# Where the weight tiles of a decoder step lie in SBUF: halves 2,176 bytes apart instead of 2,048, and three gaps

## The chip, the cores and the metric

The kernel runs on one core of a Trainium2 chip, as one program with one launch. The metric is the device time of one execution in microseconds (us); before and after are compared by the median of several executions. A profile is one further execution, recorded by the hardware profiler. Its engines are TensorE (PE for the matmuls, PEld for the weight loads that go with them), VectorE (DVE), ScalarE (ACT), GpSimd (POOL) and SyncE (SP, which here only issues DMAs). Everything is computed in 32-bit floats.

## The reference

One step of a decoder layer on 288 tokens (256 of a prompt, 32 of a sample), model width 2,048: an FFN, a mixer of two kinds of gated linear recurrences, and a second FFN, each between two RMS norms.

```python
x = x + 0.5 * rmsnorm(swiglu(rmsnorm(x, g[0]), ffn1_w_in[l], ffn1_w_out[l]), g[1])
m, sg, sh = hybrid_mixer(rmsnorm(x, g[2]), mix_w_in[l], ...)      # proj = h @ w_in; scans; merged @ w_out
x = x + rmsnorm(m, g[3])
x = x + 0.5 * rmsnorm(swiglu(rmsnorm(x, g[4]), ffn2_w_in[l], ffn2_w_out[l]), g[5])
# swiglu: gate, up = split(x @ w_in); (silu(gate) * up) @ w_out, with hidden width 5,632
```

Nearly all of the arithmetic is in the products with the weights: 2,048 x 11,264 and 5,632 x 2,048 in each FFN, about 2,048 x 7,168 and 2,048 x 2,048 in the mixer. In blocks of 128 x 128 these are 5,376 weight blocks.

## The kernel before

**Weights.** Each weight is read from memory once, in units of 1,024 columns on 128 partitions (`raw`, 512 KB). A unit holds two blocks of rows (two values of `k`), each 512 columns wide. `Weights.pieces` (L85 to L99) splits a unit into a high part `wh`, which ACT rounds to the matmul's format (L96), and a low part `wl`, the rest, which DVE subtracts (L97). 676 instructions on each engine do this over the whole kernel. The tiles come from a pool `hlp` with four buffers of each; at the two borders between stages (FFN 1 to mixer, mixer to FFN 2) some units take theirs from a second pool `hx`, on the right side of the memory, which lives only around the border.

**Products.** The activations are split in the same way into `xh` and `xl` (in the FFN's second half `hh` and `hl`). A product is then three matmuls: high by high, low by high, high by low (L591, L592, L593 in `mm3`). Each loads a 128 x 128 weight block into TensorE and streams 288 columns of a moving tile past it. 5,376 blocks by three, and 24 more at the two borders, make 16,152 weight products. In this document a *weight product* is one such matmul with its weight load.

**Order.** `block` runs over units, over the two `k` of a unit, and over four column blocks `f`: twelve weight products in a row use the tiles `xh[k]` and `xl[k]`, and the next twelve those of `k + 1`. In the last unit of a block (the *tail*) `f` is the outer loop: three products with one `k`, three with the next. A `gate` or `up` block of an FFN has sixteen `k`, so 168 products in runs of twelve and 24 in the tail; an `out` block has four `k`, 24 in two runs of twelve and 24 in the tail. The engines' order is the order in which the code issues, except where `issue_after` places instructions behind others.

**Borders.** `Fill` (from L506) holds eight pairs of early-split tiles (`xh`, `xl`, `yh`, `yl` for `k` from 0 to 3) whose products are put into the wait for the norm at each border. `Border` opens the pools for them.

**Layout.** Each partition of SBUF is one row of bytes, and pools lay their tiles one behind the other. These are the start addresses of the built program, modulo 256 bytes:

- An activation tile has 288 x 4 = 1,152 bytes, which is 4 x 256 + 128. So `xh[k]` and `xl[k]` start at 64 for even `k` and at 192 for odd `k`.
- `hh` and `hl` have four such slices in 4,608 = 18 x 256 bytes; the slices start at 0, 128, 0, 128.
- A weight tile has 4,096 bytes, and a weight block starts every 512 bytes in it. All 15,480 products with weights from `hlp` load them from 192, the 672 with weights from `hx` from 224.
- The `Fill` tiles start at 224 (high) and 96 (low).

From this follows the *difference* of a weight product, the start of its moving tile minus the start of its weight block, modulo 256:

| difference | weight products before | which |
|---|---|---|
| 0 | 5,724 | `xh`, `xl` with odd `k`, weights from `hlp` |
| 128 | 5,724 | `xh`, `xl` with even `k`, weights from `hlp` |
| 64 | 1,992 | `hh`, `hl` with even `k`, `hlp` |
| 192 | 1,992 | `hh`, `hl` with odd `k`, `hlp` |
| 32, 96, 160, 224 | 720 | weights from `hx`, `Fill` tiles |

Of the kernel before, what the change touches and what calls it, by code (L numbers as in the profile page):

```python
# [9 lines left out]
F32 = mybir.dt.float32  # L10
F32R = mybir.dt.float32r
U8 = mybir.dt.uint8
AF = mybir.ActivationFunctionType
ALU = mybir.AluOpType
PSUM = bass.MemoryType.PSUM

P = 128
TP = 256
TS = 32
T = TP + TS  # L20
# [10 lines left out]

RAW_BUFS = 3
HL_BUFS = 4
SCAN_LAG = 4
X_EARLY = 12


class Weights:
# [46 lines left out]
    def pieces(self, n):  # L85

        i = self.split
        raw = self.raws.pop(i)
        pool = self.extra if i in self.extra_units else self.hlp
        h = pool.tile([P, 1024], F32R, name=f"wh{i}", tag="wh")  # L90
        l = pool.tile([P, 1024], F32R, name=f"wl{i}", tag="wl")
        self.parts[i] = (h, l)
        self.split += 1
        for c in range(0, 1024, 1024 // n):
            c = slice(c, c + 1024 // n)
            i1 = self.nc.scalar.activation(h[:, c], raw[:, c], AF.Copy).ins  # L96
            i2 = self.nc.vector.tensor_tensor(l[:, c], raw[:, c], h[:, c].bitcast(F32), op=ALU.subtract).ins  # L97
            self.recent = i1, i2
            yield i1, i2  # L99

    def room(self):
        more = self.split in self.extra_units
        held = sum((i in self.extra_units) == more for i in range(self.used, self.split))
        return held < (2 if more else HL_BUFS)

# [21 lines left out]
def trunk_kernel(ctx, tc, x_prompt, x_sample, state_gla, state_hgrn, norm_gains, f1_in, f1_out, f2_in, f2_out,  # L127
# [3 lines left out]
    V, S, G, PE = nc.vector, nc.scalar, nc.gpsimd, nc.tensor  # L131

    const = ctx.enter_context(tc.tile_pool(name="const", bufs=1))
    xpool = ctx.enter_context(tc.tile_pool(name="xpool", bufs=1))
    rawp = ctx.enter_context(tc.tile_pool(name="rawp", bufs=RAW_BUFS))
    hlp = ctx.enter_context(tc.tile_pool(name="hlp", bufs=HL_BUFS))
    mmp = ctx.enter_context(tc.tile_pool(name="mmp", bufs=5, space=PSUM))
# [27 lines left out]
    def mmtile(name):  # L165
        return mmp.tile([P, 512], F32, name=name, tag="mm")
# [36 lines left out]
    def wider(n):  # L203

        return {i for i in range(n - 44, n + 4) if i // 2 % 3 == (n + 2) // 2 % 3}
# [37 lines left out]
    EARLY = 4  # L243
# [5 lines left out]
    rt = xpool.tile([P, T], F32, name="rt")  # L249
    rp = xpool.tile([P, T], F32, name="rp")  # L250
    acc = xpool.tile([P, T], F32, name="acc")

    def gain(i, k):
        return prm[:, i * KT + k:i * KT + k + 1]
# [218 lines left out]
    class PreNorm:  # L473
# [3 lines left out]
        def __init__(self, name, update, ahead, at):  # L477

            self.name, self.update, self.ahead, self.at, self.late = name, update, ahead, at, []
            self.tmps = None  # L480
# [25 lines left out]
    class Fill:  # L506
# [3 lines left out]
        def __init__(self, pool, name, gains, gnext, some, ahead):  # L510
            self.gnext, self.name, self.some, self.ahead = gnext, name, some, ahead

            self.gains = pool.tile([P, EARLY], F32, name=f"{name}g")
            V.tensor_tensor(self.gains, gains[:, 0:EARLY], prm[:, gnext * KT:gnext * KT + EARLY], op=ALU.mult)
            self.tiles = [[[pool.tile([P, T], F32R, name=f"{name}{n}{p}{k}") for p in "hl"] for k in range(EARLY)]
                          for n in "xy"]

        def old(self):
            for k in range(EARLY):
# [62 lines left out]
    def block(name, nk, rhs, evac, width=512, tick=None, tail=1, hold=False, most=99, fill=None, late=0):  # L582

        nf, per = width // P, 1024 // width
        nu = nk // per
        ps = [mmtile(f"{name}_{f}") for f in range(nf)]
        ws = [W.next() for _ in range(EARLY // per)] if fill else []

        def mm3(dst, w, f, k, parts, start, stop):
            c = (k % per) * width + f * P  # L590
            yield lambda: PE.matmul(dst, w[0][:, c:c + P], parts[0], start=start, stop=False)  # L591
            yield lambda: PE.matmul(dst, w[0][:, c:c + P], parts[1], start=False, stop=False)  # L592
            yield lambda: PE.matmul(dst, w[1][:, c:c + P], parts[0], start=False, stop=stop)  # L593

        def mm(w, f, k):
            if not fill or f or k >= EARLY:
                for ready in mm3(ps[f][:, 0:T], w, f, k, rhs(k), k == 0, k == nk - 1):
                    product[0] = ready().ins

        if fill:  # L600
            fill.products(lambda dst, k, parts, stop: mm3(dst, ws[k // per], 0, k, parts, k == 0, stop), ps[0][:, 0:T])
        for u in range(nu - tail):
            w = ws.pop(0) if ws else W.next()
            for k in range(u * per, (u + 1) * per):
                if fill and k < UPDATED:

                    fs = range(1 if k < EARLY else 0, nf)
                    threes = [list(mm3(ps[f][:, 0:T], w, f, k, rhs(k), k == 0, False)) for f in fs]
                    for three in threes:
                        three[0]()  # L610
                        product[0] = three[2]().ins
                    with tc.issue_after(product[0]):
                        for three in threes:
                            product[0] = three[1]().ins
                elif k < late:

                    threes = [list(mm3(ps[f][:, 0:T], w, f, k, rhs(k), k == 0, False)) for f in range(nf)]
                    for ready in [r for t in threes for r in t[:2]] + [t[2] for t in threes]:
                        product[0] = ready().ins
                else:  # L620
                    for f in range(nf):
                        mm(w, f, k)
                if tick is not None:
                    tick(k)
            W.ahead(most)
            if fill and u == 5:
                fill.scaled()
        ws = [W.next() for _ in range(tail)]
        for f in range(nf):
            for k in range((nu - tail) * per, nk):  # L630
                mm(ws[k // per - (nu - tail)], f, k)
            evac(f, fill.total(ps[f][:, 0:T]) if fill and f == 0 else ps[f][:, 0:T])
        for k in range((nu - tail) * per, nk):
            if tick is not None:
                tick(k)
        if not hold:
            W.ahead()
# [187 lines left out]
    def mixer(pn, border):  # L825
        with ExitStack() as mx:
# [588 lines left out]
            def step(k):  # L1415
                if k is not None and gens and gens[0][2] and k < SCAN_LAG:
                    return
                while gens:
                    try:
                        next(gens[0][1])  # L1420
                        return
                    except StopIteration:
                        gens.pop(0)
# [165 lines left out]
    class Border:  # L1589


        def __init__(self, n, gains, gnext, some, ahead=0):
            self.pools = ExitStack()
            W.begin_extra(self.pools.enter_context(tc.tile_pool(name=f"hx{gnext}", bufs=2, side="right")), wider(n))
            self.fill = Fill(self.pools.enter_context(tc.tile_pool(name=f"fl{gnext}", bufs=1, side="right")),
                             f"fill{gnext}", gains, gnext, some, ahead)
# [47 lines left out]
```

## Time and profile before

| | us |
|---|---|
| three executions | 2,247.73, 2,248.10, 2,248.68 |
| median | 2,248.10 |
| the profiled execution, its own time | 2,247.12 |
| its span, first instruction to last | 2,245.3 |
| around the span | 1.8 |

In the profile "busy" is the time in which an engine has an instruction under way. Matmuls overlap: a matmul of 288 columns is listed with some 295 ns, but the next one starts some 132 ns after it. So what a weight product costs is read from the distance between two starts, not from its listed duration. The timeline lists starts to 0.01 us; a run of twelve products with one moving tile is then the distance between the first product of one `k` and the first of the next, both of line L591. The span is measured from the first instruction, at 0.00.

### The profile page before, as it was taken

The numbers are of one execution on the slowest core, as the hardware profiler recorded it, in microseconds if no ns is written. First come the engines' busy times: TensorE is split into PE (matmuls) and PEld (weight loads), VectorE is DVE, ScalarE is ACT, GpSimd is POOL, SyncE is SP. The second block draws the span as 40 slices with busy tenths as digits, with TensorE's granted clock in tenths as the row PEclk, the third lists the DMA queues.
The fourth block names the chain that finished last, engine by engine and source line by source line (L and its number), as shares of the span: only waits on it lengthen the run. The fifth ranks groups of instructions, "written<-read, shape, count | busy, mean of one in ns | idle before, by whom it ended". The sixth has DMA issues, their size and how long they took to land.

```text
span 2245.3 us, 43325 instructions
## 1 busy us (share of the span) xinstructions
PE 2233.0 (99%) x17832; PEld 2218.3 (99%) x17832; DVE 1386.3 (62%) x2252; ACT 1022.8 (46%) x1556; POOL 171.2 (8%) x311
## 2 busy tenths in 40 slices
PE   9999999999999999999999999999999999999998
PEld 9999999999999999999999999999999999999998
DVE  7545545554555568888888755944555465545646
ACT  6443333333334345555676654544333333333344
POOL 2000000000000001333000000530000000000005
PEclk9999999999999999999999999999999999999999
DMA  7555555555555554667565554665555555555555
GB/s 223 171 169 162 167 168 162 168 167 163 169 165 182 170 164 141 194 197 213 174 172 169 178 184 130 195 186 164 165 169 164 165 169 164 165 169 163 166 166 152
DMA packets 226758, 384.28 MB, mean 171 GB/s; under 512 B 21106, under 2 KB 60544, under 8 KB 226560
## 3 DMA queue, kind: packets, MB, share of 16 engines
q1 hardware_dynamic: 213968, 365.15, 51.8%
q0 software_dynamic: 10416, 16.18, 2.7%
q8 instruction: 140, 2.29, 0.4%
q10 hardware_dynamic: 2176, 0.18, 0.1%
q14 instruction: 58, 0.48, 0.1%
HBM read 363.75 MB, written 11.80 MB: 167 GB/s over the span
## 4 chain that ended last, share of the span: by engine, by line
PE 99%; DVE 0%; POOL 0%; ACT 0%; issue 0%; DVEq 0%; POOLq 0%
PE gate L591 10%; PE gate L593 10%; PE gate L592 10%; PE out L592 8%; PE up L593 8%; PE up L591 8%; PE up L592 8%; PE out L593 8%; PE out L591 8%; PE hfq L591 2%; PE hfq L593 2%; PE hfq L592 2%; PE mo L593 2%; PE mo L591 2%; PE mo L592 2%; PE hi L591 1%
## 5 line engine op out<-in xcount | busy, mean ns | idle before, releaser
L97 DVE TENSOR_TENSOR wl<-raw,wh 128x1024 fp32r<-128x1024 f32 (+1 forms) x676 | 821.8, 1217 | 616.7 <-ACT wh L96 612.8
L96 ACT ACTIVATE wh<-raw 128x1024 fp32r<-128x1024 f32 (+1 forms) x676 | 711.5, 1054 | 1018.8 <-PE gate L592 308.8
L591 PE MATMUL gate<-xh,wh 128*128 128x288 f32 x1660 | 489.4, 296 | 0.0
L593 PE MATMUL gate<-xh,wl 128*128 128x288 f32 x1660 | 487.7, 295 | 0.0
L592 PE MATMUL gate<-xl,wh 128*128 128x288 f32 x1660 | 485.7, 295 | 0.0
L592 PE MATMUL out<-hl,wh 128*128 128x288 f32 x1408 | 416.1, 296 | 0.0
L593 PE MATMUL up<-xh,wl 128*128 128x288 f32 x1408 | 415.6, 295 | 0.0
L593 PE MATMUL out<-hh,wl 128*128 128x288 f32 x1408 | 415.3, 295 | 0.0
L592 PE MATMUL up<-xl,wh 128*128 128x288 f32 x1408 | 415.1, 295 | 0.0
L591 PE MATMUL up<-xh,wh 128*128 128x288 f32 x1408 | 415.0, 295 | 0.0
L591 PE MATMUL out<-hh,wh 128*128 128x288 f32 x1408 | 414.1, 294 | 0.0
L591 PEld LDWEIGHTS gate<-xh,wh 128*128 128x128 f32 x1660 | 311.3, 188 | 0.9 <-DVE z L1533 0.2
L593 PEld LDWEIGHTS gate<-xh,wl 128*128 128x128 f32 x1660 | 311.4, 188 | 0.2 <-DVE wl L97 0.2
L592 PEld LDWEIGHTS gate<-xl,wh 128*128 128x128 f32 x1660 | 310.7, 188 | 0.3
L593 PEld LDWEIGHTS out<-hh,wl 128*128 128x128 f32 x1408 | 265.0, 188 | 0.0
L591 PEld LDWEIGHTS out<-hh,wh 128*128 128x128 f32 x1408 | 264.9, 188 | 0.0
L592 PEld LDWEIGHTS out<-hl,wh 128*128 128x128 f32 x1408 | 264.7, 188 | 0.0
L593 PEld LDWEIGHTS up<-xh,wl 128*128 128x128 f32 x1408 | 264.6, 188 | 0.0
L592 PEld LDWEIGHTS up<-xl,wh 128*128 128x128 f32 x1408 | 264.4, 188 | 0.0
L591 PEld LDWEIGHTS up<-xh,wh 128*128 128x128 f32 x1408 | 264.3, 188 | 0.0
L755 DVE TENSOR_TENSOR y<-out,y 128x288 f32<-128x288 f32 x288 | 121.3, 453 | 101.3 <-PE out L593 98.3
L720 POOL DMA_DIRECT2D zT<-b x40 | 23.2, 586 | 721.7 <-issue 721.7
(396 smaller groups left out, 2573.2 us busy)
## 6 DMA issues: line engine op xcount, KB each, us to landing
raw<-in_ffn_w_in_dram SPq DMA_DIRECT2D x350, 512.0 KB, 3.5
raw<-in_ffn_w_out_dram SPq DMA_DIRECT2D x176, 512.0 KB, 3.6
raw<-in_mix_w_in_dram SPq DMA_DIRECT2D x64, 512.0 KB, 4.0
raw<-in_mix_w_in_dram SPq DMA_DIRECT2D x96, 256.0 KB, 3.2
raw<-in_mix_w_out_dram SPq DMA_DIRECT2D x32, 512.0 KB, 3.7
out_dram<-s POOLq DMA_DIRECT2D x32, 256.0 KB, 2.8
s<-in_state_gla_dram SPq DMA_DIRECT2D x16, 256.0 KB, 4.7
s<-in_state_hgrn_dram SPq DMA_DIRECT2D x16, 256.0 KB, 5.3
```

Source lines behind the costliest of these rows:

```text
L96: i1 = self.nc.scalar.activation(h[:, c], raw[:, c], AF.Copy).ins
L97: i2 = self.nc.vector.tensor_tensor(l[:, c], raw[:, c], h[:, c].bitcast(F32), op=ALU.subtract).ins
L591: yield lambda: PE.matmul(dst, w[0][:, c:c + P], parts[0], start=start, stop=False)
L592: yield lambda: PE.matmul(dst, w[0][:, c:c + P], parts[1], start=False, stop=False)
L593: yield lambda: PE.matmul(dst, w[1][:, c:c + P], parts[0], start=False, stop=stop)
L720: queues[n % len(queues)].dma_start(dst[q * TS:(q + 1) * TS, 4 * g:4 * g + 4, :, cols].rearrange("p k t c -> p (k t) c"), b32[rows, q])
L755: V.tensor_tensor(y[k], ps, y[k], op=ALU.add)
```

## The change

The weight tile gets two halves, one for each `k` of its unit, 544 instead of 512 columns apart: 32 unused columns, 128 bytes, stand behind each half. The halves start 2,176 bytes apart, and the tile takes 4,352 = 17 x 256 bytes. The split on ACT and DVE writes a pattern of 2 x 512 elements where it wrote 1,024 in a row; the pieces of 512 and 256 columns at the start are as before. A gap of 128 bytes is put behind the activations, one of 160 bytes ahead of the border's pools, the `Fill` tiles are laid out by kind (all `xh`, then all `xl`) and their gains tile is 64 wide and last.

```diff
+HALF = 512 + 32
@@ Weights.pieces
-        h = pool.tile([P, 1024], F32R, name=f"wh{i}", tag="wh")
-        l = pool.tile([P, 1024], F32R, name=f"wl{i}", tag="wl")
+        h = pool.tile([P, 2, HALF], F32R, name=f"wh{i}", tag="wh")
+        l = pool.tile([P, 2, HALF], F32R, name=f"wl{i}", tag="wl")
...
-        for c in range(0, 1024, 1024 // n):
-            c = slice(c, c + 1024 // n)
-            i1 = self.nc.scalar.activation(h[:, c], raw[:, c], AF.Copy).ins
-            i2 = self.nc.vector.tensor_tensor(l[:, c], raw[:, c], h[:, c].bitcast(F32), op=ALU.subtract).ins
+        raw = raw.rearrange("p (a b) -> p a b", b=512)
+        for j in range(n):
+            a = slice(0, 2) if n == 1 else slice(2 * j // n, 2 * j // n + 1)
+            w = min(512, 1024 // n)
+            c = slice(j * w % 512, j * w % 512 + w)
+            i1 = self.nc.scalar.activation(h[:, a, c], raw[:, a, c], AF.Copy).ins
+            i2 = self.nc.vector.tensor_tensor(l[:, a, c], raw[:, a, c], h[:, a, c].bitcast(F32), op=ALU.subtract).ins
@@ trunk_kernel
     acc = xpool.tile([P, T], F32, name="acc")
+    xpool.tile([P, 32], F32, name="gap")
@@ Fill
-            self.gains = pool.tile([P, EARLY], F32, name=f"{name}g")
+            tiles = [[[pool.tile([P, T], F32R, name=f"{name}{n}{p}{k}") for k in range(EARLY)] for p in "hl"] for n in "xy"]
+            self.tiles = [list(zip(*hl)) for hl in tiles]
+            self.gains = pool.tile([P, 64], F32, name=f"{name}g")[:, 0:EARLY]
...
-            self.tiles = [[[pool.tile([P, T], F32R, name=f"{name}{n}{p}{k}") for p in "hl"] for k in range(EARLY)]
-                          for n in "xy"]
@@ block, mm3
-            c = (k % per) * width + f * P
-            yield lambda: PE.matmul(dst, w[0][:, c:c + P], parts[0], start=start, stop=False)
+            a, c = k % per, slice(f * P, f * P + P)
+            yield lambda: PE.matmul(dst, w[0][:, a, c], parts[0], start=start, stop=False)
...
@@ Border
+            top = self.pools.enter_context(tc.tile_pool(name=f"top{gnext}", bufs=1, side="right"))
+            top.tile([P, 40], F32, name=f"gap{gnext}")
```

In the built program the activation tiles stay where they were. The first half of every weight tile, in both pools, starts at 64 modulo 256 and the second at 192; `hh` and `hl` slices start at 128, 0, 128, 0; the `Fill` tiles at 64 for even and 192 for odd `k`. So the differences become 0 for 11,928 weight products and 64 for 4,224, and no other occurs. Where one `k` ends and the next begins, the weights of the new half are loaded while the last moving tile of the old `k` is still being streamed; between these two the difference is 128 in 1,331 places and 192 in 848.

Every engine issues the same instructions in the same order as before. Because other tiles now share bytes with the border's pools, four waits name another instruction: GpSimd's clearing of `vs` in the mixer's setup (L879 before) now waits for a product of the first border, the clearing of `qm` no longer waits for ACT, and two waits of SP, ahead of the first recurrent state's load and of the copies into `zT`, are for products that stand six and three places later.

More of the change, by code (lines that the diff above doesn't have):

```diff
@@ L589, in mm3 @@
         def mm3(dst, w, f, k, parts, start, stop):
-            c = (k % per) * width + f * P
-            yield lambda: PE.matmul(dst, w[0][:, c:c + P], parts[0], start=start, stop=False)
-            yield lambda: PE.matmul(dst, w[0][:, c:c + P], parts[1], start=False, stop=False)
-            yield lambda: PE.matmul(dst, w[1][:, c:c + P], parts[0], start=False, stop=stop)
+            a, c = k % per, slice(f * P, f * P + P)
+            yield lambda: PE.matmul(dst, w[0][:, a, c], parts[0], start=start, stop=False)
+            yield lambda: PE.matmul(dst, w[0][:, a, c], parts[1], start=False, stop=False)
+            yield lambda: PE.matmul(dst, w[1][:, a, c], parts[0], start=False, stop=stop)
         def mm(w, f, k):
```

## The prediction

> **What bounds the kernel now.** I read the page first, then the chain of waits, then the timeline of TensorE. The page's engine line, the engines' shares of the chain that ended last, and one stretch of 200 us in the view by windows (us, then busy time and count of PE, PEld, DVE, ACT, POOL; granted clock; DMA share and GB/s):
>
> ```profile
> span 2245.3 us, 43325 instructions
> PE 2233.0 (99%) x17832; PEld 2218.3 (99%) x17832; DVE 1386.3 (62%) x2252; ACT 1022.8 (46%) x1556; POOL 171.2 (8%) x311
> ...
> PE 99%; DVE 0%; POOL 0%; ACT 0%; issue 0%; DVEq 0%; POOLq 0%
> ...
> 300.00:500.00 200.00, 200.00 (x1512) 200.00 (x1511) 107.24 (x144) 75.53 (x87) 0.00 (x0) 1.00 0.52 164
> ...
> PE warm L306 <- POOL onesD L229: 1.1, 1, 1.1
> PE postf L432 <- DVE sq L422: 0.2, 1, 0.2
> ```
>
> TensorE is the chain, 99% of it, at full granted clock, and the two longest lines of what PE waited for come to 1.3 us. In the stretch, which holds weight products only, 1,512 of them take 200 us: 132.3 ns each. 16,152 at that price are 2,137 us of 2,245. So the time can fall only if the distance from start to start falls, and what lengthens it is not a wait that the profile names.
>
> The timeline shows that this distance is not one number. Here are the first products of successive `k` (L591) in an `up` block of FFN 1, each twelve products after the one above (start, duration, engine, line):
>
> ```profile
> 395.26 0.30 PE L591 MATMUL up<-xh,wh 128*128 128x288 f32 x1
> ...
> 396.86 0.29 PE L591 MATMUL up<-xh,wh 128*128 128x288 f32 x1
> ...
> 398.44 0.29 PE L591 MATMUL up<-xh,wh 128*128 128x288 f32 x1
> ...
> 400.05 0.29 PE L591 MATMUL up<-xh,wh 128*128 128x288 f32 x1
> ...
> 401.62 0.30 PE L591 MATMUL up<-xh,wh 128*128 128x288 f32 x1
> ...
> 403.22 0.29 PE L591 MATMUL up<-xh,wh 128*128 128x288 f32 x1
> ...
> 404.80 0.29 PE L591 MATMUL up<-xh,wh 128*128 128x288 f32 x1
> ...
> 414.34 0.30 PE L591 MATMUL up<-xh,wh 128*128 128x288 f32 x1
> ...
> 417.54 0.29 PE L591 MATMUL out<-hh,wh 128*128 128x288 f32 x1
> ```
>
> The first row is `k` = 2. Even `k` take 1.60, 1.61 and 1.60 us, odd `k` 1.58, 1.57 and 1.58: some 25 ns more for twelve equal instructions on equal data, always with the same sign. Even `k` have the difference 128, odd `k` 0. The last two rows bound the tail: 24 products with the two differences three by three take 3.20 us, 133.3 each.
>
> Is it the difference, or the parity of `k`? At the first border weights from `hx` start 32 bytes higher. Then even `k` have 96 and odd `k` 224:
>
> ```profile
> 776.94 0.30 PE L591 MATMUL up<-xh,wh 128*128 128x288 f32 x1
> ...
> 780.12 0.30 PE L591 MATMUL up<-xh,wh 128*128 128x288 f32 x1
> ...
> 781.71 0.30 PE L591 MATMUL up<-xh,wh 128*128 128x288 f32 x1
> ...
> 783.31 0.29 PE L591 MATMUL up<-xh,wh 128*128 128x288 f32 x1
> ...
> 784.89 0.30 PE L591 MATMUL up<-xh,wh 128*128 128x288 f32 x1
> ...
> 786.49 0.29 PE L591 MATMUL up<-xh,wh 128*128 128x288 f32 x1
> ...
> 788.09 0.29 PE L591 MATMUL up<-xh,wh 128*128 128x288 f32 x1
> ```
>
> From 780.12 to 786.49 the weights are from `hx`, and the order turns round: even `k` 1.59 and 1.58, odd `k` 1.60 and 1.60. From 786.49 they are from `hlp` again, and even `k` takes 1.60. The moving tiles are the same. So it is where the two lie to each other.
>
> Read over the whole trace, from the first weight product to the last (16,152 of them, matched in order with the built program's addresses, intervals over 160 ns left out), the distance to the next start is 131.8 ns at difference 0 (5,635 intervals), 133.45 at 128 (5,615), 131.9 at 64 (1,991), 132.7 at 192 (1,992), and 133.0 over the four others (709). The first and the last:
>
> ```profile
> 6.38 0.38 PE L591 MATMUL gate<-xh,wh 128*128 128x288 f32 x1
> ...
> 2231.63 0.30 PE L593 MATMUL out<-hh,wl 128*128 128x288 f32 x1
> ```
>
> The mean of all is 132.55. Sorted by whether DVE, ACT or DMAs are busy beside it, 128 stays 0.9 to 2.6 ns above 0 in every group of some size, so another engine's traffic does not make it.
>
> **The change part by part.** The differences become 0 and 64 everywhere, so the slow classes take the fast price:
>
> - difference 128: 5,724 x (133.45 - 131.8) = 9.5 us;
> - difference 192: 1,992 x (132.7 - 131.9) = 1.6 us;
> - the 720 others: 720 x (133.0 - 131.8) = 0.8 us.
>
> Together 11.9 us, all on the path that sets the end.
>
> *Less, at the change of `k`.* In 2,179 places the moving tile of the old `k` meets the load of the new half, at 128 or 192. The trace before does not show single meetings between long stretches at difference 0. If each costs as its class does: 1,331 x 1.65 + 848 x 0.8 = 2.9 us. If they cost nothing: 0. For nothing speaks that the first product behind a turn from 0 to 128 has 133.1 (599) and behind a turn back 130.7 (634): a pair of turns averages 131.9. I take 1.0.
>
> *More, in the tails.* In threes between threes at 128, difference 0 itself has 133.0 (243 runs of the tails like the one above). After the change two of three in a tail are at 0 and one is a meeting. About 730 products at 0 stand in such tails: between 0 and 730 x 1.2 = 0.9 us. I take 0.6.
>
> *The split.* ACT and DVE write 2 x 512 instead of 1,024 in a row, 670 times each. The rows by shape (busy us, mean ns), the same lines on 512 columns from the start-up, and a DVE product whose pattern is broken into many pieces by the code:
>
> ```profile
> L97 DVE TENSOR_TENSOR wl<-raw,wh 128x1024 fp32r<-128x1024 f32 x670 | 818.9, 1223 | 616.7 <-ACT wh L96 612.8 <-PE tp_k L926 1.0 <-PE hms L1346 0.3
> L1104 DVE TENSOR_TENSOR Q<-Q,F 128x256 f32<-128x256 f32 x30 | 12.7, 422 | 4.4 <-PE sc L1044 4.0 <-ACT R L1119 0.3
> ...
> L97 DVE TENSOR_TENSOR wl<-raw,wh 128x256 fp32r<-128x256 f32 x4 | 1.5, 419 | 0.0
> L97 DVE TENSOR_TENSOR wl<-raw,wh 128x512 fp32r<-128x512 f32 x2 | 1.4, 688 | 0.0
> ...
> 1000.00:1100.00 100.00, 100.00 (x1085) 96.23 (x1084) 87.55 (x202) 64.60 (x150) 22.39 (x36) 1.00 0.65 190
> 1000.00:1100.00 100.00, 28.21 (x24) 1.00 0.65 190
> ```
>
> At worst a broken pattern costs as two instructions, 2 x 688 = 1,376 against 1,223, so 153 ns more; at best nothing. The broken L1104 takes 422 where the unbroken 256 columns take 419: I take 0. Either way it is covered: in DVE's busiest 100 us (87.55 busy, 24 splits, the last row) the worst adds 24 x 0.153 = 3.7 us and leaves 8.7 idle. Without that cover a late split would hold up a weight load, at most 670 x 0.153 = 103 us.
>
> *The waits.* GpSimd clears `vs` in the second of these rows, long after the product that it now waits for, which ends the border's first group (first row):
>
> ```profile
> 853.82 0.30 PE L593 MATMUL qk<-fill2xh,wl 128*128 128x288 f32 x1
> ...
> 874.72 1.01 POOL L879 MEMSET vs<- 128x512 f32 x2
> ```
>
> 20 us of cover; behind it on GpSimd's queue stand the loads of the gate's weights, which are not delayed. SP's two waits move by six and three products, 0.8 and 0.4 us, at transfers that are wanted many products later. I take 0 for all, with 1 us as the other end.
>
> Sum: 11.9 - 1.0 + 0.6 = 11.5 us. The profiled execution takes 2247.1, 1.0 under the median of the three; the median should fall from 2248.1 to 2236.6. The least of this working is 11.9 - 2.9 - 1.0 = 8.0 us, 2240.1. The most is every product at the price of a long run at difference 0, 131.55 over 348 unbroken twelves: 16,152 x 1.0 = 16.2 us, 2231.9.
>
> [...]
>
> **The rivals.**
>
> *Less than half of it (2240 to 2244).* A meeting could cost more than its own interval: in the tails, products at difference 0 that stand between threes at 128 take 133.0. If the three behind each of the 1,331 meetings at 128 also lose 1.2 ns, that is 1,331 x (1.65 + 3.6) + 848 x 0.8 = 7.7 us, and 11.9 - 7.7 = 4.2 us remain: 2243.9. For it: the tail's 3.20 us. Against: behind a turn to 0, the first product is fast at once, 130.7.
>
> *No change (2245 to 2248).* The difference may not be what counts, but a pair of starts. Before, weights start at 192 or 224 only; 64 was never seen. If a moving tile at 64 with weights at 64 stays at 133.45, the 9.5 us are lost and 2.4 remain: 2245.7. [...] Against: three kinds of moving tiles and two of weights sort by the difference.
>
> *Slower.* If weights that start at 64 are slow with every moving tile, half of all products pay. The highest class of the trace is difference 32, with 133.7 over its 146 intervals and 134.3 over the first 24 of them. Half at 134.3 and half at 131.8 is 133.05, 0.5 over now: 16,152 x 0.5 = 8.1 us, 2256.2. It turns to a loss from 133.3 on. For it only that this start is untried; against it the same sorting.
>
> **How the numbers follow.** Forecast 0.71 (2232 to 2240, likeliest 2236.6), less than half 0.14, no change 0.08, slower 0.07. A measurement of this kernel tells 0.2% from no change, 4.5 us, so faster is below 2243.6: 0.71 + 0.14 less a little for the rival's edge, 0.84; same 0.09; slower 0.07. The range that holds 8 of 10 reaches from the most of the sum to the middle of the first rival: 2231.5 to 2243.0.
>
> **What would show it.** Right: in the same `up` block, even and odd `k` both at 1.57 to 1.58 us; some 1,521 products in 200 us of an FFN where 1,512 stood; the tails under 3.20 us; L97 near 1,223 ns. Even `k` still at 1.60 with odd at 1.58 would show that a pair of starts counts. A tail of 3.20 would show that the meetings spoil their neighbours. A DVE line of L97 near 1,376 and PE waits for `wl` beyond the few tenths now would show the split on the path. The forecast is wrong if the median stays above 2240.

## The result, and the profile after

| | before | after |
|---|---|---|
| median, us (range, executions) | 2,248.14 (2,247.73 to 2,248.68, 6) | 2,238.28 (2,238.03 to 2,240.27, 6) |
| ratio, 95% interval | | 0.9958 [0.9945, 0.9970] |
| the profiled execution, its span | 2,247.12, 2,245.3 | 2,238.78, 2,237.0 |

The change saves 9.9 us of the 11.5 predicted. A later profile of the same kernel, called `again` below, has a span of 2,235.5, so the two profiled spans fall by 8.3 and 9.8 us.

First the span, the engines' line and the stretch of 200 us of weight products, in the order of columns of the prediction:

```profile
span 2237.0 us, 43324 instructions
...
PE 2223.4 (99%) x17832; PEld 2207.6 (99%) x17832; DVE 1385.9 (62%) x2252; ACT 1022.0 (46%) x1556; POOL 171.2 (8%) x311
...
300.00:500.00 200.00, 200.00 (x1519) 200.00 (x1518) 109.19 (x148) 75.56 (x87) 0.00 (x0) 1.00 0.55 166
```

TensorE still sets the end (95% of the chain that ended last is its own), at the same granted clock, 1.00, and DVE and ACT are busy for the same time as before (1,386.3 and 1,022.8 us then). 1,519 products go through where 1,512 did: 131.7 ns each instead of 132.3.

The timeline of TensorE in the same `up` block of FFN 1 (start, duration, engine, line). The rows are the first products of `k` = 0 to 4, twelve products apart, then the first of the tail, then the first of the next block:

```profile
390.03 0.29 PE L596 MATMUL up<-xh,wh 128*128 128x288 f32 x1
...
391.62 0.30 PE L596 MATMUL up<-xh,wh 128*128 128x288 f32 x1
...
393.21 0.30 PE L596 MATMUL up<-xh,wh 128*128 128x288 f32 x1
...
394.80 0.30 PE L596 MATMUL up<-xh,wh 128*128 128x288 f32 x1
...
396.39 0.29 PE L596 MATMUL up<-xh,wh 128*128 128x288 f32 x1
...
412.29 0.30 PE L596 MATMUL up<-xh,wh 128*128 128x288 f32 x1
...
415.48 0.29 PE L596 MATMUL out<-hh,wh 128*128 128x288 f32 x1
```

Even and odd `k` are now alike, as the prediction asked. But both take 1.59 us, not 1.57 to 1.58: the dear twelves came down from 1.60 and the cheap ones went up. The tail takes 3.19 us, hardly less than the 3.20 before.

Read over the whole trace as in the prediction (distance to the next start, intervals over 160 ns left out), in ns:

| products | intervals | before | after | again |
|---|---|---|---|---|
| with `xh`, `xl` | some 11,640 | 132.60 | 132.11 | 132.08 |
| with `hh`, `hl` | some 4,220 | 132.37 | 131.17 | 131.18 |

In the profile after, that is 0.49 x 11,640 = 5.7 us from `xh` and `xl`, and 1.20 x 4,220 = 5.1 us from `hh` and `hl`, 10.8 together. The span fell by 8.3. The rest is in intervals over 160 ns between two weight products. They sum to 22.4 us before (97 of them) and 25.7 after (106). The nine more would have taken 1.2 us as common ones, so 2.2 us are lost there. 0.3 went among the other matmuls, and 10.8 - 2.2 - 0.3 = 8.3. In `again` the gain is 6.1 + 5.0; 0.35 is lost in 99 such intervals, 0.3 among the other matmuls, and its first weight product starts 0.5 later, which leaves the 9.8 within rounding.

Two of these intervals, 0.96 us from 1,438.8 us on (the start of the second `gate` block of FFN 2) and 0.71 us from 719.7 on (an `out` block of FFN 1), make 1.4 of the 2.2: (0.96 - 0.13) + (0.71 - 0.13). They have rows in the view of what PE waited for, after (us in total, times, longest):

```profile
PE gate L596 <- DVE u L679: 0.7, 1, 0.7
PE out L596 <- DVE u L679: 0.4, 1, 0.4
PE qk L596 <- DVE y L984: 0.2, 1, 0.2
```

In `again` the first two are gone from the same view:

```profile
PE warm L311 <- POOL onesD L233: 1.1, 1, 1.1
PE qk L596 <- DVE y L984: 0.2, 1, 0.2
```

The same kernel has these waits in one execution and not in another, so they are no standing cost of the change.

The split, by the view of groups with shapes kept apart (busy us, mean ns, idle before and its releasers):

```profile
L101 DVE TENSOR_TENSOR wl<-raw,wh 128x1024 fp32r<-128x1024 f32 x670 | 818.9, 1223 | 612.4 <-ACT wh L100 609.3 <-PE tp_k L931 0.5 <-PE hms L1351 0.3
L100 ACT ACTIVATE wh<-raw 128x1024 fp32r<-128x1024 f32 x670 | 708.2, 1058 | 1010.3 <-PE gate L597 303.8 <-PE out L597 264.5 <-PE up L597 250.1
```

2 x 512 elements take 1,223 ns on DVE, as 1,024 in a row did, and 1,058 on ACT, where those took 1,059.

GpSimd's clearing of `vs`, beside the last product of the border's first group, in the timeline:

```profile
849.71 0.29 PE L598 MATMUL qk<-fill2xh,wl 128*128 128x288 f32 x1
...
870.62 1.01 POOL L884 MEMSET vs<- 128x512 f32 x2
```

It starts 20.9 us after the product that it must wait for: the wait is covered.

### The profile page after: what moved, and what is told of

Same layout as the page of the kernel before. It is cut to its first block, busy times and chain, and to the rows that moved or that the text cites. A ratio compares the mean times of both kernels' runs of the same rounds, so it can differ in the third digit from the quotient of the medians.

```text
span 2237.0 us, 43324 instructions
## 1 busy us (share of the span) xinstructions
PE 2223.4 (99%) x17832; PEld 2207.6 (99%) x17832; DVE 1385.9 (62%) x2252; ACT 1022.0 (46%) x1556; POOL 171.2 (8%) x311
## 3 DMA queue, kind: packets, MB, share of 16 engines
q10 hardware_dynamic: 2176, 0.18, 0.1%
## 4 chain that ended last, share of the span: by engine, by line
PE 95%; DVE 2%; DMA 1%; ACT 1%; issue 1%; POOL 0%; DVEq 0%; ACTq 0%; POOLq 0%
PE gate L596 9%; PE gate L598 9%; PE gate L597 9%; PE out L597 8%; PE out L596 8%; PE out L598 8%; PE up L598 8%; PE up L597 8%; PE up L596 8%; PE hfq L596 2%; PE mo L598 2%; PE hfq L598 2%; PE hfq L597 2%; PE mo L597 2%; PE mo L596 2%; PE hi L596 1%
```

## The experiments

All medians in us; "x" and "h" are the mean distance, in ns, from start to start of the products with `xh`, `xl` and with `hh`, `hl`, read over the whole trace. Kernels with one time have had one execution.

| kernel | median (range, executions) | before beside it | ratio, 95% interval | x | h |
|---|---|---|---|---|---|
| `again` (the changed kernel) | 2,237.99 (2,237.27 to 2,238.23, 4) | 2,248.37 | 0.9955 [0.9940, 0.9970] | 132.08 | 131.18 |
| `d128` | 2,247.67 (2,246.70 to 2,248.56, 10) | 2,248.37 | 0.9997 [0.9988, 1.0006] | 132.98 | 131.20 |
| `d192` | 2,247.74 (1) | 2,247.79 | | 133.06 | 131.13 |
| `d32` | 2,252.21 (1) | 2,247.79 | | 133.45 | 131.18 |
| `d64` | 2,230.52 (2,229.70 to 2,232.43, 5) | 2,248.37 | 0.9922 [0.9910, 0.9935] | 131.41 | 131.13 |
| `d96` | 2,231.34 (1) | 2,247.79 | | 131.47 | 131.15 |
| `d96b` (the same kernel) | 2,232.33 (2,231.26 to 2,232.48, 4) | 2,248.34 | 0.9927 [0.9911, 0.9944] | 131.48 | 131.15 |
| `nomeet` | 2,238.80 (2,237.96 to 2,239.57, 4) | 2,248.37 | 0.9958 [0.9945, 0.9972] | 131.69 | 132.30 |
| `nomeet64` | 2,238.80 (2,237.68 to 2,240.06, 4) | 2,247.79 | 0.9960 [0.9940, 0.9980] | 131.75 | 132.28 |
| `threes0` | 2,241.37 (2,240.57 to 2,242.14, 4) | 2,248.63 | 0.9968 [0.9954, 0.9983] | 132.69 | 130.22 |
| `threes64` | 2,229.95 (2,227.27 to 2,240.45, 6) | 2,248.63 | 0.9915 [0.9901, 0.9928] | 131.94 | 132.22 |
| `threes64b` (the same kernel) | 2,227.36 (2,226.75 to 2,228.13, 4) | 2,248.34 | 0.9907 [0.9892, 0.9922] | 131.19 | 131.11 |

**Is it the difference?** In the `d` kernels everything of the change stays: the padding, the split in halves, the pools. Only the sizes of the three gaps change, so that every weight tile starts some bytes lower (in `d192` 64 bytes higher), and the number in the name is the difference that `xh` and `xl` then have with the weights. At the change of `k` the difference is 128 more (modulo 256). `hh` and `hl` keep their 64, with meetings at 192. `d128`, against the changed kernel:

```diff
-    xpool.tile([P, 32], F32, name="gap")
...
-            self.gains = pool.tile([P, 64], F32, name=f"{name}g")[:, 0:EARLY]
+            self.gains = pool.tile([P, 32], F32, name=f"{name}g")[:, 0:EARLY]
...
-            top.tile([P, 40], F32, name=f"gap{gnext}")
+            top.tile([P, 72], F32, name=f"gap{gnext}")
```

The other `d` kernels have other widths in the same three places: 24, 56, 48 in `d32`; 16, 48, 56 in `d64`; 8, 40, 64 in `d96`; 48, 16, 88 in `d192`.

> The changed kernel with the gap behind the activations taken out and the border's gap and gains tile resized, so that all weights lie 128 bytes lower modulo 256: every product of xh and xl (11,880) at difference 128, the meetings at the change of k at 0; hh and hl stay at 64. Padding, split in 2 x 512 and order stay. Theory that the difference sets the price: these products take 133.3 to 133.5 ns instead of 132.1, time 2238.3 + 11,880 x 1.3 ns = 2253 to 2254 us, slower than before. Rival that the saving came from the padding itself or another part of the change: 2238 us.

> The changed kernel with gaps so that xh and xl stand at 32 and meet 160; hh and hl at 64. Theory that the few products at 32 before show its price (133.7 in 146 intervals): xh and xl at 133.4 to 133.8, 2253 to 2258 us. Rival that those 146 were dear because they stand at a border, and that prices between 0 and 64 are like those of 0 and 64: 131.5 to 132.1, 2231 to 2238 us.

> The changed kernel with gaps so that xh and xl stand at 192 and meet 64 at the change of k; hh and hl at 64. Theory that what a difference costs in stretches of twelve before holds (192 took 132.7, in twelves 133.2): xh and xl at 132.6 to 133.2 ns, 11,880 x 0.5 to 1.1 = 6 to 13 us over the changed kernel, 2244 to 2251 us. Rival that 192 is cheap, as its meetings in the kernel with 64 everywhere (129.2): 131.4 or less, 2230 us.

`d128` ends at 0.9997 of before, and this is a balance of two things: `xh` and `xl` at 132.98 are some 4.4 us dearer than before (132.60), and `hh` and `hl`, which keep their 64, are some 4.9 us cheaper (131.20 against 132.37). It stayed 5 to 6 us under the 2,253 to 2,254 expected. Most of that is in `xh` and `xl`: the expectation put all of them at 133.3 to 133.5, while the meetings, now at difference 0, have 131.22 (1,304 intervals) and the others 133.21. The view by windows of `d128`:

```profile
300.00:500.00 200.00, 200.00 (x1512) 200.00 (x1512) 107.02 (x144) 75.67 (x87) 0.00 (x0) 1.00 0.55 164
```

These are as many products as before, 1,512, with the padding in place. `d192` came out within its expectation (133.06 ns, 2,247.74 us). `d32` has the price expected (133.45 ns) and ends at 2,252.21, just under the 2,253 to 2,258 expected and 4.4 us above before; both had one execution. The view of `d32`:

```profile
300.00:500.00 200.00, 200.00 (x1508) 200.00 (x1507) 105.89 (x142) 75.68 (x87) 0.00 (x0) 1.00 0.50 164
```

So the gain comes from where the moving tile and the weights lie to each other; the runs show no part of it that comes from the padding or the split by themselves. `hh` and `hl` answer the rival that a pair of starts counts: over `again` and the five kernels `d32` to `d192` their weights start at all eight multiples of 32 modulo 256, the difference stays 64, and the price stays at 131.13 to 131.20. The same instructions in the same order take from 2,230.5 to 2,252.2 us by the layout alone: `xh` and `xl` have 131.41 ns in `d64` and 133.45 in `d32`. What makes the one dearer than the other, no run here shows.

**Is 0 the best difference?** `d64` and `d96` ask it.

> The changed kernel with gaps resized so that all weights lie 64 bytes lower: every weight product at difference 64, all meetings at 192. Theory that 64 with meetings at 192 is a cheaper place than 0 with meetings at 128, as out products show in the changed kernel (131.5 ns in twelves, 130.8 in tails, against 132.06 and 132.6 for gate and up): 10,400 x 0.55 + 1,480 x 1.8 = 8.4 us less than the changed kernel, 2230 us. Rival that out products are cheaper for another reason (their moving tile, their place): xh and xl products stay at 132.1, time 2238 us.

> The changed kernel with gaps so that xh and xl stand at 96 and meet 224; hh and hl at 64. Theory that prices of before hold (96: 131.9 in 215 intervals, 224: 133.3): xh and xl at 132.0 to 132.2, 2237 to 2239 us. Rival that 96 is as good as 64 in this layout (131.4): 2230 us.

> The kernel with xh and xl at 96, timed: its one execution was at 2231.34. Theory that 96 with meetings at 224 is as good as 64 with meetings at 192: 2230.5 to 2232 us, and a profile with xh and xl at 131.5 ns. Rival that it was one good execution: 2235 us or more.

`d64` came out where it was expected, 7.5 us under the changed kernel on the same chip, and the ranges do not touch. In `d64` the same `up` block starts and comes to its tail here, 168 products apart:

```profile
388.57 0.29 PE L596 MATMUL up<-xh,wh 128*128 128x288 f32 x1
...
410.65 0.29 PE L596 MATMUL up<-xh,wh 128*128 128x288 f32 x1
```

22.08 us are 131.4 ns each; in the changed kernel the same 168 products take 412.29 - 390.03 = 22.26, 132.5 each. Two things differ between these two kernels, 64 against 0 and meetings at 192 against meetings at 128. `nomeet` and `nomeet64` take them apart.

`d96` was expected too high, and its rival came: `xh` and `xl` have 131.47. Its meetings, at 224, were taken as dear, and they have 131.36 (1,303 intervals, in `d96b`), less than the 131.49 of the rest. The second measurement confirms the time.

**What do the meetings cost?** `nomeet` puts `xh` and `xl` at 0 without any meeting: it is the kernel before, with the activation tiles padded instead of the weights.

```diff
+TW = 320
...
-    xh = [xpool.tile([P, T], F32R, name=f"xh{k}") for k in range(KT)]
-    xl = [xpool.tile([P, T], F32R, name=f"xl{k}") for k in range(KT)]
     rt = xpool.tile([P, T], F32, name="rt")
+    xh = [xpool.tile([P, TW], F32R, name=f"xh{k}")[:, 0:T] for k in range(KT)]
+    xl = [xpool.tile([P, TW], F32R, name=f"xl{k}")[:, 0:T] for k in range(KT)]
...
+            top = self.pools.enter_context(tc.tile_pool(name=f"top{gnext}", bufs=1, side="right"))
+            top.tile([P, 8], F32, name=f"gap{gnext}")
```

`hh` and `hl` stay at 64 and 192 by turns, as before. `nomeet64` is the same with `rt` where it was, a gap of 16 columns behind the activations and one of 56 at the border: all `xh`, `xl` at 64.

> The kernel before with xh and xl tiles 1,280 bytes apart instead of 1,152, rt laid out ahead of them and 32 bytes above the border's pools: every product of xh and xl at difference 0, and none meets another difference at the change of k. Weights unpadded, split in one row of 1,024; hh and hl alternate 64 and 192 as before. Theory that the meetings at 128 keep the changed kernel's twelves at 132.06 instead of the 131.65 that difference 0 has between the other twelves before: xh and xl at 131.55 to 131.7 ns, tails too; against the changed kernel 11,880 x 0.45 + 1,480 x 0.5 = 6.1 us less there and 2,045 x 1.0 + 1,950 x 1.4 = 4.8 us more on hh and hl: 2237 us. Rival that a meeting costs nothing and the 132.06 has another cause: 132.0 to 132.1 ns, 2243 us.

> As the kernel without meetings (xh and xl tiles 1,280 bytes apart, weights unpadded), with gaps that put xh and xl at difference 64 instead of 0, none meeting another difference; hh and hl alternate 64 and 192. Theory that the meetings at 192 are a help in the kernel with 64 everywhere (129.2 ns in the meeting itself, 131.7 in the rest): without them xh and xl stand at 131.7 to 131.9, time 2238 to 2240 us. Rival that 64 is cheaper than 0 by itself: 131.4 or less, 2235 us.

In `nomeet` the same 168 products:

```profile
390.34 0.29 PE L592 MATMUL up<-xh,wh 128*128 128x288 f32 x1
...
412.46 0.29 PE L592 MATMUL up<-xh,wh 128*128 128x288 f32 x1
```

22.12 us, 131.67 each, and over the whole trace the twelves have 131.68 and the threes in the tails 131.67: without meetings there is one price. The changed kernel has the same difference with meetings, and 132.08 to 132.11. So the 1,304 meetings at 128 cost 0.39 to 0.42 x 11,640 = 4.5 to 4.9 us, 3.5 to 3.7 ns each. Counted in TensorE's order in the built program, the changed kernel has 1,324 meetings at 128 and 842 at 192; the 1,331 and 848 given with the change are a little high, which moves no figure here.

Where the cost lies is seen by place. A single interval says little, because the intervals of a stream repeat in a pattern of four: in `nomeet`, without any meeting, the fifth to the eighth of a twelve have 130.8, 130.8, 130.6 and 134.4 ns. So the twelve intervals are averaged in fours; the last one of the twelve is the meeting where there is one (721 or 722 unbroken twelves of `xh` and `xl` in each kernel):

| kernel | first four, behind the change of `k` | middle four | last four |
|---|---|---|---|
| `nomeet` (0, no meeting) | 131.72 | 131.65 | 131.68 |
| the changed kernel (0, meetings at 128) | 132.12 | 131.72 | 132.32 |
| `nomeet64` (64, no meeting) | 131.69 | 131.73 | 131.73 |
| `d64` (64, meetings at 192) | 130.96 | 131.70 | 131.62 |

Away from the meetings, in the middle four, all four kernels have the same price to 0.08 ns. A meeting at 128 costs in its own four and again in the four behind it. A meeting at 192 saves in the four behind it: (131.75 - 131.41) x 11,640 = 4.0 us, some 3 ns each. The 129.2 ns that the expectations read off the meetings of `d64` are not their doing: in its twelves the fourth and the eighth interval, which are no meetings, have 127.9 and 128.0, the twelfth 127.8, and in `nomeet64` the same three places have 128.3, 128.4 and 128.4.

`nomeet` has the price expected for `xh` and `xl` and ends at the changed kernel's time (2,237 was expected, 2,238.80 measured), though its `xh` and `xl` are 4.7 us cheaper, because its `hh` and `hl` are dearer: (132.30 - 131.18) x 4,220 = 4.7 us. `nomeet64` came out as expected, at 131.75 and 2,238.80.

**Were the pauses the change's?** `again` is the changed kernel, profiled once more.

> The changed kernel once more, for its waits and its time on this chip. In its first profile TensorE stood longer than before in three places: near 723 us (0.74 us more), 1260 us (0.33 us) and 1443 us (0.88 us), on DVE by the view of waits. Theory that DVE's chains there were just in time before and are now too late: the three pauses come back within 0.2 us, time 2238 us. Rival that they were late transfers of that one execution: they are gone or stand elsewhere, and the profiled execution is 1.5 to 2 us shorter, 2236 to 2237 us.

In the profile after, the three pauses lie at 719.7, 1,255.7 and 1,438.8 us. The first was not there again. At the second, six intervals take 0.91 us in `again`, against 1.05 in the kernel before and 1.37 after. At the third, four take 0.77, against 0.59 before; the long one among them had 0.96 us in the profile after and has 0.26 here, and over the other kernels it lies anywhere up to 1.17 us (`nomeet`), with 1.06 in `d128` and 0.51 in `d64`. So most of the 2.2 us belongs to that one execution, as the rival had it; what makes such a pause come and go was not followed further.

**More meetings.** If meetings at 192 beside 64 shorten the stream, more of them should shorten it more; meetings at 128 beside 0 should do the reverse. `threes64` is `d64`, and `threes0` the changed kernel, with `k` as the inner loop where nothing else is woven in, as it is in the tails: three products with one `k`, three with the next.

```diff
-            for k in range(u * per, (u + 1) * per):
+            if tick is None and not fill and not late:
+                for f in range(nf):
+                    for k in range(u * per, (u + 1) * per):
+                        mm(w, f, k)
+            for k in range(u * per, (u + 1) * per) if tick is not None or fill or late else ():
```

> The kernel with 64 everywhere, and in blocks without work tied to k (most of the FFNs, the mixer's output) the column block f is the outer loop in every unit, k the inner: three products with one k, three with the next, as in the tails, so 4,564 meetings at 192 instead of 2,166. Theory that a meeting at 192 makes the products around it cheaper by some 3 ns: threes cost 130.9 instead of 131.4 for xh and xl and about as much less for hh and hl: 7,392 x 0.5 + 2,045 x 0.6 = 4.9 us less than 2230.5, 2225.6 us. Rival that the tails are cheaper for their place at a block's end: 2230.5 us.

> The changed kernel (0 and 64) with the same loop order: 3,158 meetings at 128 instead of 1,331. Theory that a meeting at 128 costs: threes at 132.6 instead of 132.06 for xh and xl, 7,392 x 0.55 = 4.1 us more, and hh and hl (64 with 192) 1.3 us less: 2241 us. Rival that the loop order alone gains or loses, whatever the meetings: 2233 us as the other kernel of this pair, or 2238.

> The kernel with 64 everywhere and threes once more, because its profiled execution took 2240.45 us while its five others took 2227 to 2231. Theory that its products can settle into more than one rhythm, and that the profiled execution was in a dearer one: a profile near 2229 us now shows xh and xl at 130.9 to 131.4 ns and hh and hl at 130.3 to 131.2, where that one had 131.9 and 132.2. Rival that being profiled costs this kernel 10 us: the profile is at 2240 again.

`threes0` ends at the time expected, 2,241, by two errors that cancel. Its 3,138 meetings at 128 have 133.78 and its threes with `xh` and `xl` 132.92, not 132.6: against the changed kernel `xh` and `xl` lose 6.8 to 7.1 us, not 4.1, and `hh` and `hl` gain 4.0, not 1.3. The 1,834 meetings more cost 3.7 to 3.9 ns each, near the 3.5 to 3.7 found above, so that price is met a second time.

`threes64` is the quickest kernel of the study, but its expectation did not hold: 2,225.6 was expected, and its medians are 2,229.95 and, timed again as `threes64b`, 2,227.36. In neither profile are `hh` and `hl` cheaper than in `d64` beyond 0.02 ns, and `xh` and `xl` are cheaper in the second alone. So it is not shown that more meetings at 192 shorten the stream more.

Nor does this kernel have one time. Five of the six executions of `threes64` took 2,227.27 to 2,230.76 us; the profiled one took 2,240.45. Profiled again (`threes64b`), the same kernel took 2,226.75, so being profiled does not by itself cost the 10 us; `xh` and `xl` at 131.19 and `hh` and `hl` at 131.11 are what its theory of a cheaper rhythm expected. A stretch in FFN 1 and one in FFN 2, `threes64`:

```profile
300.00:500.00 200.00, 200.00 (x1515) 200.00 (x1514) 108.54 (x147) 75.77 (x88) 0.00 (x0) 1.00 0.55 166
...
1800.00:2000.00 200.00, 200.00 (x1515) 200.00 (x1514) 108.15 (x145) 74.38 (x84) 0.00 (x0) 1.00 0.56 167
```

And the same view of `threes64b`:

```profile
300.00:500.00 200.00, 200.00 (x1541) 200.00 (x1540) 111.60 (x153) 76.58 (x88) 0.00 (x0) 1.00 0.56 169
...
1800.00:2000.00 200.00, 200.00 (x1515) 200.00 (x1514) 104.39 (x136) 74.27 (x83) 0.00 (x0) 1.00 0.55 167
```

One and the same program runs through FFN 1 at 1,541 products in 200 us (129.8 ns) or at 1,515 (132.0), at the same granted clock and nearly the same DMA share. What chooses is open. It also shows that the difference and the meetings do not settle the price in this loop order: `hh` and `hl` have difference 64 and meetings at 192 in all three profiles, and 130.22 in `threes0`, 132.22 in `threes64` and 131.11 in `threes64b`.

## Why the prediction was right, point by point

- **TensorE's pace is set by the difference, not by the parity of `k` or another engine.** Right: even and odd `k` are equal after the change (1.59 us for twelve), and `d128` and `d32` take the gain back with gaps alone (2,247.67 and 2,252.21 us). The difference to the weights that are loaded *next*, beside the stream under way, counts as well. In the profile after, the load for the product at 396.39 us, the first of its `k`, is listed from 396.26 for 0.19 us, and the last product of the old `k` from 396.25 for 0.29. And in the changed kernel every `xh` and `xl` product is at 0 itself, and still the fours around a meeting have 132.32 and 132.12 where the middle four have 131.72.
- **The sum of 11.5 us.** The measured 9.9 lies inside the range, but that it came so near is luck: two terms were off and nearly cancelled. By the prediction's own terms, `xh` and `xl` stood for 9.5 + 0.3 (their share of "the others") - 0.8 (theirs of the meetings) + 0.6 (tails) = 9.6 us, and `hh` and `hl` for the remaining 1.9. Measured were 5.7 to 6.1 and 5.0 to 5.1.
- **Less, at the change of `k`: 1.0 taken, 2.9 the bound.** This is the step that failed. Those at 128 alone cost 4.5 to 4.9 us. The step let a meeting cost its own interval at most, at its class's price; in fact the four intervals behind it are lengthened too (132.12 against the 131.72 of the middle four). What spoke for nothing, the first products behind a turn in the kernel before, could not tell: there the weights from `hlp` all start at 192, so a turn between two of them is no meeting, and the difference to the next weights is the product's own.
- **More, in the tails: 0.6.** It did not come. Over the 1,509 intervals of such tails the products with `xh` and `xl` have 132.65 after against 133.24 before, so 0.9 us in all, where the class terms (1.2: half of them from 133.45 to 131.8) and this 0.6 make 1.8. The prediction said that a tail of 3.20 us would show that the meetings spoil their neighbours; 3.19 was measured, and `nomeet`, with 131.67 in the tails, shows it.
- **Difference 192 to 64: 1.6.** Too small. The class price of 64 before, 131.9, was that of stretches between stretches at 192. All at 64, with meetings at 192, took 131.17. `xh` and `xl` at 64 without meetings have 131.75 (`nomeet64`); if that holds for `hh` and `hl`, about half of their 5 us is the difference 64 by itself, and the rest would be the meetings'. No run has `hh` and `hl` at 64 without meetings, so this share is an estimate.
- **The split: 0, at worst 153 ns an instruction.** Right: 1,223 and 1,223 ns.
- **The waits: 0, at most 1.** Right as far as the traces tell: GpSimd has 20.9 us of cover, and in `again` the view of what TensorE waited for has the same waits as before, so SP's moved waits cost nothing that shows there. The two new waits of PE, 0.7 and 0.4 us, were in one profile and not in the next.
- **The rivals.** "No change" and "slower" fell: in the changed kernel's twelves, weights at 64 with moving tiles at 64 have 132.06, weights at 192 with tiles at 192 132.02. "Less than half" named what the fours show, a meeting that costs its neighbours (132.12 behind it), priced at 5.2 ns against the 3.5 to 3.7 found. By its terms `xh` and `xl` would have given 2.8 us and `hh` and `hl` 1.4; they gave 5.7 to 6.1 and 5.0 to 5.1, so it fell on both.

What stays open: why the price goes by the difference, counted here modulo 256 bytes. The runs show 0, 64 and 96 cheap (132.11, 131.41 and 131.47 ns), and 32, 128 and 192 dear (133.45, 132.98 and 133.06), for `xh` and `xl`, each with meetings at 128 more; counted modulo 512, the products of `nomeet` at 0 and at 256 have 131.71 and 131.67, so those two are alike. Nothing here shows the mechanism.

## What to carry to other kernels

Where matmuls with a weight load each follow one another without a wait and the pace still varies, sort the distances from start to start by where the moving tile and the next weights lie to each other. Then try two or three offsets by gaps in the layout: here they moved the time by 1% (2,230.5 to 2,252.2 us) with no instruction changed, and the offset that looked best before (0) was not the best. By themselves 0 and 64 cost the same (131.69 and 131.75 without meetings); the meetings that came with each made the difference (132.11 and 131.41 with them). Price a layout by a whole stream with that layout, not by class means out of a mixed one.

## What the runs showed of the hardware

- A single odd pair in a long stream moved more than its own interval, and in either direction: +3.5 to 3.7 ns for each meeting at 128 in a stream at 0, where its own four intervals had 132.32 and the four behind 132.12 against 131.72 in the middle; 131.41 against 131.75 ns for the whole stream with and without meetings at 192 beside 64. In threes the second does not repeat: with some 3,140 meetings at 192, `xh` and `xl` had 131.94 in one profile and 131.19 in the next.
- A stream held one of two paces for hundreds of microseconds: `threes64`, from 100 to 700 us in FFN 1, 129.8 ns in one profile (1,540 to 1,541 products in each 200 us) and 132.0 in the other (1,515), and 2,226.75 or 2,240.45 us for the whole. Of the ten executions measured, one took over 2,231 us. Neither of the two profiles has both FFNs at 129.8. For a kernel that must be steady, `d64`, 2,230.52 with 2.7 us from lowest to highest, is the better choice of the two; both beat the kernel before and the change.
